# Two heads per step in a fixed TensorE order, and scores of the banded heads on all 128 rows

## The chip, the core and the metric

The kernel runs on one core of a Trainium2 chip. The metric is the device time of one execution in microseconds (us), the median of three runs. A run is followed by an execution under the hardware profiler, and the profile and the trace come from that one.

## What is computed

Two transformer blocks over 512 tokens of width 1024, in float32: a first block of two layers, then a second block of two layers which also carries 256 context tokens. The stages that matter here are the attention stages:

```python
# first block, each layer: 4 output heads, each over three dilated key sets; pooled and convolved branches beside them
br_a = multiscale_pool(a_in, pool_w[l], pool_scale[l]) @ w_branch_a[l]
br_b = (b_b * causal_dwconv(b_c * b_x, conv_b_w[l])) @ w_branch_b[l]
br_c = dilated_attention(q, k, v) @ w_branch_c[l]
# second block, layer 0: heads "a" (8 query heads, 2 key heads, banded, with a sink) and "b" (difference of two softmaxes)
s_loc = jnp.where(valid, einsum('bnqhgd,bnkhd->bhgnqk', qb, kb) * scale, NEG_INF)   # own block and its neighbours
s_ctx = einsum('bnqhgd,bchd->bhgnqc', qb, k_ctx) * scale
p_loc, p_ctx, _ = joint_softmax(s_loc, s_ctx, s_sink)
outs = einsum('bhqk,bkhd->bqhd', p[:, 0] - lam * p[:, 1], v)
# second block, layer 1: 16 latent heads over 768 keys (mla_attend)
```

## The kernel before

Every product of float32 data is made of three matmuls on two float32r parts, a high and a low one: high by high, low by high, high by low (`mm3`, lines 133 to 138). A head of the first three kinds is 64 wide, so a query block's scores contract over 64 of the array's 128 rows: rows 0 to 63 for one head, 64 to 127 for its neighbour.

An attention stage is a list of items, each a tuple of four functions: `qk` (scores into a PSUM tile S, two banks, and the row minimum on VectorE), `soft` (exponentials on ScalarE, normalisation on GpSimd), `tr` (`probs_T`, line 421: six or fewer TensorE transposes into two T tiles, the first copied out by ScalarE, the second by VectorE) and `pv` (probabilities by values, `pv_pair` for two heads side by side). `pipeline` (line 382) walks over the list with a delay for each function, and after each step lets a generator of other work (`Fill`, line 41) emit projections up to a budget of so many nanoseconds. `Fill.need` emits what is left of a piece that the next item needs. PSUM has eight banks: two S tiles, two T tiles of one bank and two "p" tiles of one bank, and the p tiles are shared by the projections, their transposes and the outputs of `pv`.

The order in which TensorE meets these instructions is not the one of the program: the framework's scheduler picks, from what it expects to be ready, by priority.

There are four such stages, in the order of time:

- `mix1` (lines 604 to 690), once in each layer of the first block: 16 items (two groups of heads p, four query blocks, two heads each), with the projections of the second group (`proj1`), the pooled branch (`pool_in`, `pool_out`) and the convolved branch as fill, in this order. `pool_in` goes through a chain on GpSimd and VectorE (lines 565 to 590); `pool_out` multiplies its results.
- the difference heads of `mix_ab` (`diff_items`): four heads h, each eight items over 768 keys (four query blocks, two maps m) and two items over the 256 context keys, with the projections `proj_ab` of the heads and of the banded groups 4 and 5 as fill.
- the banded heads of `mix_ab` (`window_items`): 32 items of two or three local blocks and two context blocks, then eight context items, with hardly any fill left (200 ns a step).
- `mix_mla`: 64 items with its own projections `proj_mla` as fill, 96 rows per head.

Of the kernel before, what the change touches and what calls it, by code (L numbers as in the profile page):

```python
# [78 lines left out]
class Net:  # L79
# [398 lines left out]
    def items1(self, p, g, fill, oT):  # L478
# [5 lines left out]
        def item(b, h):  # L484
            st = {}
            rows = slice(64 * h, 64 * h + 64)
            qs = slice(b * P, (b + 1) * P)

            def qk():
                if (b, h) == (0, 0):  # L490
                    fill.need(p)
                q0, k0, q12, k12 = g["q0"], g["k0"], g["q12"], g["k12"]
                ps = self.psum("S")
                self.mm3(ps[:, 0], (q0[rows, 0, qs], q0[rows, 1, qs]), (k0[rows, 0], k0[rows, 1]), True, True)
                for j in range(2):
                    o = ps[:, 1, j * P : (j + 1) * P]
                    mm(o, lhsT=q12[rows, j, qs], rhs=k12[rows, j, qs], start=True, stop=True)
                st["s"] = ps.rearrange("p a b -> p (a b)")[:, :768]
                st["nm"] = self.nmax(st["s"], mask=self.mask1[:, b])

            def soft():
                st["P"], r = self.exps(st["s"], st["nm"], 768)
                self.norm_probs(st["P"], r)

            def tr():
                sh[b, h] = self.probs_T(st["P"], 6)

            def pv():
# [7 lines left out]
                self.pv_pair(o, [sh[b, 0], sh[b, 1]], vs)  # L516
                self.copy(oT[:, qs], o)

            return (qk, soft, tr, pv if h else None)

        return [item(b, h) for b in range(4) for h in range(2)]
# [506 lines left out]

# [683 lines left out]
```

## Time and profile before

| what | us |
|---|---|
| runs | 3593.20, 3593.13, 3589.31 (median 3593.13) |
| the profiled execution, its own time | 3594.31 |
| its span, first to last instruction | 3592.5 |
| TensorE busy in the span | 3519.9 (98%) |
| VectorE, ScalarE, GpSimd busy | 1917.2 (53%), 1335.5 (37%), 429.1 (12%) |
| mean granted TensorE clock | 0.994 |

A matmul's duration in the trace goes from its start to a modelled end, and the next one starts before that end; what a matmul costs TensorE in a dense stretch is the distance between two starts. The 1.8 us between span and time lie outside the program's instructions.

### The profile page before, as it was taken

What the parts mean: (1) busy time and instruction counts of PE and PEld (TensorE: products, weight loads), DVE (VectorE), ACT (ScalarE), POOL (GpSimd) and SP (SyncE); (2) the same over time, 40 slices, a digit from 0 to 9 for tenths busy, and PEclk for the clock granted to TensorE, in tenths of its full rate; (3) what the DMA queues carried; (4) which work ended last, traced back from release to release, by engine and by line L of the source; (5) the groups of instructions that cost most, each with busy time, mean ns of one, the idle gap of its engine ahead of it and who ended that gap; (6) DMA issues with size and microseconds to landing.
All of it is one profiled execution on the core that took longest, in us unless ns stands there. A gap on an engine that the chain in (4) does not pass through costs nothing.

```text
span 3592.5 us, 48260 instructions
## 1 busy us (share of the span) xinstructions
PE 3519.9 (98%) x19261; PEld 2994.1 (83%) x19261; DVE 1917.2 (53%) x3018; ACT 1335.5 (37%) x2372; POOL 429.1 (12%) x572
## 2 busy tenths in 40 slices
PE   8999999999999999999999999999999989999998
PEld 8877798888898778888878887888888878888887
DVE  4453357466534335666766666536663466753243
ACT  4432344332443324532344446332111356643222
POOL 0211111000102111200011122200000122220001
PEclk9999999999999999999999999999999999999999
DMA  4233334344322433354431112335443121022232
GB/s 129 83 129 94 100 112 141 106 144 135 103 66 93 135 94 124 121 167 150 131 107 40 36 48 77 125 93 168 132 132 103 46 80 33 25 89 87 90 102 86
DMA packets 110130, 364.02 MB, mean 101 GB/s; under 512 B 16617, under 2 KB 18209, under 8 KB 109905
## 3 DMA queue, kind: packets, MB, share of 16 engines
q1 hardware_dynamic: 109904, 360.94, 31.7%
q8 instruction: 151, 2.47, 0.3%
q14 instruction: 75, 0.61, 0.1%
HBM read 347.16 MB, written 13.73 MB: 100 GB/s over the span
## 4 chain that ended last, share of the span: by engine, by line
PE 90%; DVE 3%; ACT 2%; POOL 2%; DMA 1%; issue 1%; SPq 0%; ACTq 0%; POOLq 0%; DVEq 0%
PE ps L136 21%; PE ps L137 21%; PE ps L138 21%; PE p L136 4%; PE p L137 4%; PE p L138 4%; PE T L430 3%; PE p L444 3%; PE S L136 2%; PE S L137 1%; PE S L138 1%; DMA adaw<-in_ada_w_dram 1%; PE T L138 1%; PE T L136 1%; PE T L137 1%
## 5 line engine op out<-in xcount | busy, mean ns | idle before, releaser
L112 DVE TENSOR_TENSOR wlo<-raw,whi 128x1024 fp32r<-128x1024 f32 (+2 forms) x510 | 603.8, 1190 | 734.6 <-ACT whi L109 719.3
L109 ACT ACTIVATE whi<-raw 128x1024 fp32r<-128x1024 f32 (+2 forms) x510 | 518.1, 1019 | 1113.1 <-PE ps L137 710.2
L137 PE MATMUL ps<-hTlo,whi 128*128 128x512 f32 (+1 forms) x2048 | 757.6, 370 | 4.1 <-DVE hTlo L177 4.0
L136 PE MATMUL ps<-hThi,whi 128*128 128x512 f32 (+1 forms) x2048 | 757.7, 371 | 2.7 <-ACT hThi L109 1.4
L138 PE MATMUL ps<-hThi,wlo 128*128 128x512 f32 (+1 forms) x2048 | 756.7, 370 | 0.0
L136 PEld LDWEIGHTS ps<-hThi,whi 128*128 128x128 f32 x2048 | 385.8, 189 | 73.0 <-issue 3.5
L137 PEld LDWEIGHTS ps<-hTlo,whi 128*128 128x128 f32 x2048 | 386.5, 189 | 69.9 <-DVE hTlo L177 4.5
L138 PEld LDWEIGHTS ps<-hThi,wlo 128*128 128x128 f32 x2048 | 386.3, 189 | 65.2
L930 DVE SCALAR_TENSOR_TENSOR acc<-adaw,cs,acc 128x1024 f32<-128x1024 f32 x168 | 209.4, 1279 | 14.6 <-DMA adaw<-in_ada_w_dram 14.3
L136 PE MATMUL ps<-whi,a 128*128 128x512 f32 x440 | 170.9, 392 | 0.7 <-ACT a L109 0.7
L138 PE MATMUL ps<-whi,a 128*128 128x512 f32 x440 | 170.6, 390 | 0.0
L137 PE MATMUL ps<-wlo,a 128*128 128x512 f32 x440 | 170.6, 390 | 0.0
L136 PE MATMUL p<-whi,hThi 128*128 128x384 f32 x464 | 163.1, 352 | 7.5 <-ACT hThi L175 3.1
L137 PE MATMUL p<-wlo,hThi 128*128 128x384 f32 x464 | 158.2, 341 | 4.7 <-DVE wlo L112 4.7
L154 POOL TENSOR_SCALAR rstd<-ms 128x1 f32<-128x1 f32 x78 | 24.1, 309 | 1137.9 <-ACT junk L152 1122.7
L138 PE MATMUL p<-whi,hTlo 128*128 128x384 f32 x464 | 158.2, 341 | 0.7 <-DVE hTlo L112 0.7
L262 DVE TENSOR_TENSOR y<-y,ps 128x1024 f32<-128x1024 f32 x88 | 106.6, 1218 | 85.7 <-PE ps L138 85.4
L136 PE MATMUL ps<-whi,act 128*128 128x512 f32 x352 | 138.2, 395 | 0.0
L137 PE MATMUL ps<-wlo,act 128*128 128x512 f32 x352 | 137.2, 392 | 0.0
L138 PE MATMUL ps<-whi,act 128*128 128x512 f32 x352 | 136.3, 390 | 0.0
L420 POOL TENSOR_SCALAR g<-g,den 128x768 f32<-128x768 f32 (+3 forms) x88 | 74.6, 850 | 424.3 <-DVE den L416 375.6
L109 ACT ACTIVATE PT<-T 128x384 f32<-128x384 f32 (+2 forms) x160 | 74.4, 465 | 111.6 <-PE T L430 109.6
(407 smaller groups left out, 6830.8 us busy)
## 6 DMA issues: line engine op xcount, KB each, us to landing
raw<-in_ffn_w_dram SPq DMA_DIRECT2D x132, 512.0 KB
adaw<-in_ada_w_dram SPq DMA_DIRECT2D x96, 512.0 KB
raw<-in_w_up_dram SPq DMA_DIRECT2D x88, 512.0 KB
raw<-in_w_gate_dram SPq DMA_DIRECT2D x48, 512.0 KB
raw<-in_w_down_dram SPq DMA_DIRECT2D x44, 512.0 KB
raw<-in_w_qkv_dram SPq DMA_DIRECT2D x48, 384.0 KB
xd<-x SPq DMA_DIRECT2D x20, 512.0 KB
raw<-in_w_conv_dram SPq DMA_DIRECT2D x18, 512.0 KB
```

What stands on the lines that cost most here:

```text
L109: return self.nc.scalar.activation(out, in_, AF.Copy, scale=scale)
L112: return self.nc.vector.tensor_tensor(out, a, b, op=ALU.subtract)
L136: mm(ps, lhsT=l[0], rhs=r[0], start=first, stop=False)
L137: mm(ps, lhsT=l[0], rhs=r[1], start=False, stop=False)
L138: mm(ps, lhsT=l[1], rhs=r[0], start=False, stop=last)
L154: nc.gpsimd.tensor_scalar(r, ms, 1.0, EPS, op0=ALU.mult, op1=ALU.add)
L262: self.nc.vector.tensor_tensor(yps[t], yps[t], y, op=ALU.add)
L420: self.nc.gpsimd.tensor_scalar(Pt, Pt, r, 1.0, op0=ALU.mult, op1=ALU.mult)
L430: nc.tensor.transpose(ps[:, k * P : (k + 1) * P], Pt[:, (k0 + k) * P : (k0 + k + 1) * P], self.ident)
L444: self.nc.tensor.matmul(o[64 * h : 64 * h + 64], lhsT=vs(h, k), rhs=PTs[h][:, k], start=k == 0, stop=k == nk - 1)
L930: nc.vector.scalar_tensor_tensor(acc[r], w, c, acc[r], op0=ALU.mult, op1=ALU.add)
```

## The change

In all stages that use `pipeline`, TensorE now gets its instructions in the order in which the program emits them (`manual_schedule`). Within a step the order of the four functions is pv, qk, tr, soft, where it was qk, tr, soft, pv. An item may carry delays of its own.

In `mix1` and in the difference heads one item now covers both heads (both maps), and the matmuls of the two alternate, rows 0 to 63 and rows 64 to 127 in turn (`mm3_two`). The two context items of a difference head become one. In `mix1` the projections of the second group are no longer fill: they are emitted in one piece ahead of that group's first scores; the convolved branch comes first in the fill and the pooled one last. In `mix_ab` each projection is added to the fill when the head before it begins, and the last one with the last context item.

In the banded heads the two parts of a query lie one above the other: rows of the head's own half hold the high part, the other half the low part (`stacked`). The keys stand in two copies, one for each key head, each with the high part in both halves of one plane, and the low part in both halves of the other (`keys_twice`). Two matmuls over 128 rows then give the scores in place of three over 64; the low by low product is added by this.

`mix_mla` and its items are not edited, but go through the same `pipeline`.

```diff
+    def mm3_two(self, pss, ls, rs):
+        for i, j in ((0, 0), (0, 1), (1, 0)):
+            for ps, l, r in zip(pss, ls, rs):
+                self.nc.tensor.matmul(ps, lhsT=l[i], rhs=r[j], start=(i, j) == (0, 0), stop=i == 1)
...
     def pipeline(self, items, fill, ns, steps=(0, 1, 2, 3)):
-        for i in range(len(items) + steps[-1]):
-            for s in (0, 2, 1, 3):
-                j = i - steps[s]
-                if 0 <= j < len(items) and items[j][s] is not None:
-                    items[j][s]()
-            fill.run(ns if isinstance(ns, (int, float)) else ns[min(i, len(items) - 1)])
+        own = [it[4] if len(it) > 4 else steps for it in items]
+        with self.tc.manual_schedule(engines={mybir.EngineType.PE}):
+            for i in range(max(j + o[3] for j, o in enumerate(own)) + 1):
+                for s in (3, 0, 2, 1):
+                    for j, it in enumerate(items):
+                        if j + own[j][s] == i and it[s] is not None:
+                            it[s]()
+                fill.run(ns if isinstance(ns, (int, float)) else ns[min(i, len(items) - 1)])
...
             def qk():    # items1
-                if (b, h) == (0, 0):
-                    fill.need(p)
+                if b == 0 and p:
+                    drain(proj)
...
-                self.mm3(ps[:, 0], (q0[rows, 0, qs], q0[rows, 1, qs]), (k0[rows, 0], k0[rows, 1]), True, True)
+                pss = [self.psum("S") for _ in both]
+                self.mm3_two([ps[:, 0] for ps in pss], [(q0[r, 0, qs], q0[r, 1, qs]) for r in both], [(k0[r, 0], k0[r, 1]) for r in both])
...
-                fill.add(1, self.proj1(l, 1, hT, gs[1], ("p",)))
+                proj = self.proj1(l, 1, hT, gs[1], ("p",))
+                fill.add("conv", self.conv_branch(l, hT, bF))
                 fill.add("pool", self.pool_in(l, hT, pooled))
-                fill.add("conv", self.conv_branch(l, hT, bF))
                 fill.add("pool", self.pool_out(l, pooled, aF))
-                self.pipeline(self.items1(0, gs[0], fill, oF[0]) + self.items1(1, gs[1], fill, oF[1]), fill, 7200, (0, 1, 2, 3))
+                items = self.items1(0, gs[0], None, oF[0]) + self.items1(1, gs[1], proj, oF[1])
+                self.pipeline(items, fill, [9000] * 4 + [8500] * 4, (0, 0, 1, 2))
...
+    def stacked(self, tok, col, tiles, dst, scale, tag):
+        tiles = list(tiles)
+        n = len(tiles) * P
+        yield 0.0
+        ps = self.psum(tag)[:, :n]
+        for j, t in enumerate(tiles):
+            self.nc.tensor.transpose(ps[:, j * P : (j + 1) * P], tok[:, t, col : col + P], self.ident)
+            yield 109
+        c = slice(tiles[0] * P, tiles[0] * P + n)
+        for h in range(2):
+            own, other = slice(64 * h, 64 * h + 64), slice(64 - 64 * h, 128 - 64 * h)
+            self.copy(dst[own, h, c], ps[own], scale=scale)
+            self.nc.vector.scalar_tensor_tensor(dst[other, h, c], ps[own], scale, f32(dst[own, h, c]), op0=ALU.mult, op1=ALU.subtract)
...
+    def keys_twice(self, g):
+        ks = (self.qk.tile([P, 2, 768], R, name="qk"),
+              self.work.tile([P, 6, 256], R, name="tok").rearrange("p a b -> p (a b)").rearrange("p (a b) -> p a b", a=2))
+        for tiles in ((4, 5), range(4)):
...
+            for kv, k in enumerate(ks):
+                own, other = slice(64 * kv, 64 * kv + 64), slice(64 - 64 * kv, 128 - 64 * kv)
+                self.split(k[own, 0, c], k[own, 1, c], ps[own])
+                self.copy(k[other, 0, c], ps[own])
+                self.sub(k[other, 1, c], ps[own], f32(k[own, 0, c]))
+        g["k", 0], g["k", 1] = ks
...
-            return (qk, soft, tr if m else None, (lambda: finish(t, 6)) if m else None)
+            return (qk, soft, tr, lambda: finish(t, 6), (0, 0, 2, 3))
...
+        def scores(ps, c, kv, q, keys):
+            k = g4["k", kv]
+            for i in range(2):
+                self.nc.tensor.matmul(ps, lhsT=qs(c)[:, kv, q], rhs=k[:, i, keys], start=i == 0, stop=i == 1)
...
-                self.mm3(ps[:, 0, c0:], ql, (kT[rows, 0, k0 * P : k1 * P], kT[rows, 1, k0 * P : k1 * P]), True, True)
-                self.mm3(ps[:, 1, :256], ql, (kT[rows, 0, 512:], kT[rows, 1, 512:]), True, True)
+                scores(ps[:, 0, c0:], c, kv, q, slice(k0 * P, k1 * P))
+                scores(ps[:, 1, :256], c, kv, q, slice(512, 768))
...
-                for i in range(1, 6):
-                    fill.add(i, self.proj_ab(hT, i, gs[i], ("p",)))
+                proj = [(i, self.proj_ab(hT, i, gs[i], ("p",))) for i in range(1, 6)]
                 items = []
                 for h in range(4):
-                    items += self.diff_items(h, gs[h], fill, oB[h])
+                    items += self.diff_items(h, gs[h], fill, oB[h], proj[h])
+                qk5 = items[-1][0]
+
+                def last():
+                    qk5()
+                    fill.add(*proj[4])
+                    fill.add(5, self.keys_twice(gs[4]))
+
+                items[-1] = (last,) + items[-1][1:]
                 n, oT = len(items), []
                 items += self.window_items(gs[4], gs[5], fill, oB, oT)
-                self.pipeline(items, fill, [3000] * n + [200] * (len(items) - n), (0, 1, 4, 5))
+                self.pipeline(items, fill, [6000] * 20 + [200] * (len(items) - n), (0, 1, 4, 5))
```

## Rows read from the trace of the kernel before

**Rows 1.** The page: busy time of each engine, share of the span.
```profile
PE 3519.9 (98%) x19261; PEld 2994.1 (83%) x19261; DVE 1917.2 (53%) x3018; ACT 1335.5 (37%) x2372; POOL 429.1 (12%) x572
...
PE 90%; DVE 3%; ACT 2%; POOL 2%; DMA 1%; issue 1%; SPq 0%; ACTq 0%; POOLq 0%; DVEq 0%
```

**Rows 2.** The four stages: stretch, length, busy time by engine, clock, DMA.
```profile
73.00:250.00 177.00, 174.26 (x1021) 148.49 (x1021) 79.60 (x159) 69.53 (x119) 31.94 (x43) 0.99 0.29 91
...
1903.00:2128.00 225.00, 220.77 (x1310) 196.37 (x1311) 140.10 (x343) 90.07 (x227) 36.84 (x64) 1.00 0.12 37
...
2140.00:2231.00 91.00, 89.78 (x731) 69.54 (x729) 65.20 (x251) 61.13 (x196) 30.83 (x48) 1.00 0.06 16
2949.00:3175.00 226.00, 222.91 (x1903) 195.98 (x1903) 157.46 (x333) 146.12 (x314) 60.03 (x64) 1.00 0.11 35
```

**Rows 3.** TensorE in order of time, a head's scores in mix1: start, duration.
```profile
201.76 0.49 PE L136 MATMUL S<-qk 64*128 64x512 f32 x1
...
202.33 0.39 PE L138 MATMUL S<-qk 64*128 64x512 f32 x1
202.56 0.60 PE L497 MATMUL S<-qk 64*128 64x128 f32 x4
203.10 0.87 PE L430 MATMUL T<-ident,g 128*128 128x128 f32 x6
```

**Rows 4.** TensorE in order of time, one map's scores, and a context item's.
```profile
1908.87 0.50 PE L136 MATMUL S<-qk 64*128 64x512 f32 x1
...
1910.11 0.44 PE L136 MATMUL p<-whi,hThi 128*128 128x384 f32 x1
...
1942.95 0.39 PE L136 MATMUL S<-qk 64*128 64x256 f32 x2
...
1943.29 0.28 PE L138 MATMUL S<-qk 64*128 64x256 f32 x2
1943.51 1.60 PE L1068 MATMUL p<-v,PT 128*128 128x128 f32 x12
```

**Rows 5.** TensorE in order of time, two banded items' scores.
```profile
2176.45 0.44 PE L136 MATMUL S<-qk 64*128 64x384 f32 x1
...
2177.53 0.77 PE L430 MATMUL T<-ident,big 128*128 128x128 f32 x5
...
2199.41 0.38 PE L136 MATMUL S<-qk 64*128 64x256 f32 x1
...
2200.31 0.66 PE L430 MATMUL T<-ident,g 128*128 128x128 f32 x4
```

**Rows 6.** The last pooled chain of layer 0: ScalarE, GpSimd, VectorE, in order of time.
```profile
174.44 0.57 ACT L109 ACTIVATE t<-p 128x512 f32<-128x512 f32 x1
...
180.09 1.03 POOL L578 TENSOR_TENSOR t<-t 128x504 f32<-128x504 f32 x1
...
182.21 0.75 DVE L586 SCALAR_TENSOR_TENSOR t<-t,poolc,t 128x512 f32<-128x512 f32 x1
```

**Rows 7.** Two stretches inside mix1: length, busy time by engine, clock.
```profile
126.00:129.00 3.00, 1.82 (x13) 1.40 (x11) 2.88 (x7) 1.99 (x5) 1.73 (x1) 1.00 0.31 42
129.00:132.40 3.40, 3.40 (x12) 3.00 (x13) 0.73 (x3) 1.64 (x4) 0.91 (x2) 0.50 0.29 118
```

**Rows 8.** Evacuations of transposes: count, min/median/max ns; then mix1's rotation.
```profile
L109 ACT ACTIVATE qk<-p x24: 377/412/633, 1902.1 to 2133.4; 128x256 fp32r<-128x256 f32 x13, 128x512 fp32r<-128x512 f32 x11
L120 DVE SCALAR_TENSOR_TENSOR qk<-p,qk x24: 406/423/693, 1902.8 to 2134.0; 128x256 fp32r<-128x256 f32 x13, 128x512 fp32r<-128x512 f32 x11
...
L458 DVE TENSOR_TENSOR ropeA<-tok,cos 128x96 f32<-128x96 f32 x8 | 2.1, 258 | 18.1 <-ACT tok L109 18.1
```

**Rows 9.** An undisturbed pv, then two behind their own item's transposes: start, duration, idle.
```profile
203.90 1.53 PE L444 MATMUL p<-PT,vt 128*64 128x128 f32 x24
...
248.66 0.55 PE L444 MATMUL p<-PT,vt 128*64 128x128 f32 x6 [0.90 <-ACT PT L109]
...
3170.95 1.89 PE L444 MATMUL p<-PT,v 128*64 128x128 f32 x24
```

More of the change, by code (lines that the diff above doesn't have):

```diff
@@ L514, in vs @@
                     return v[:, k if k < 4 else b, c : c + 64]
-                self.pv_pair(o, [sh[b, 0], sh[b, 1]], vs)
+                self.pv_pair(o, sh[b], vs)
                 self.copy(oT[:, qs], o)
-            return (qk, soft, tr, pv if h else None)
-        return [item(b, h) for b in range(4) for h in range(2)]
+            return (qk, soft, tr, pv)
+        return [item(b) for b in range(4)]
     def shifts(self, dst, src, k):
@@ L1043, in proj_ab, with diff_items @@
         sc = -(64 ** -0.5)
-        lst = [("a", tok, 0, sc), ("b", tok, P, 1.0 if i < 4 else sc)] + ([("c", v, 0, 1.0)] if i == 4 else [])
+        lst = [("a", tok, 0, sc), ("b", tok, P, 1.0 if i < 4 else sc)]
         for n, src, col, s in lst:
             g[n] = self.qk.tile([P, 2, 768], R, name="qk")
-            yield from self.transposed(src, col, (4, 5), g[n], s, tag=tags[0])
-            yield from self.transposed(src, col, range(4), g[n], s, tag=tags[-1])
+            to = self.transposed if i < 4 else self.stacked
+            yield from to(src, col, (4, 5), g[n], s, tag=tags[0])
+            yield from to(src, col, range(4), g[n], s, tag=tags[-1])
         g["v"] = v
-    def diff_items(self, h, g, fill, oB):
+    def keys_twice(self, g):
+        ks = (self.qk.tile([P, 2, 768], R, name="qk"),
+              self.work.tile([P, 6, 256], R, name="tok").rearrange("p a b -> p (a b)").rearrange("p (a b) -> p a b", a=2))
+        for tiles in ((4, 5), range(4)):
+            n = len(tiles) * P
+            yield 0.0
+            ps = self.psum("p")[:, :n]
+            for j, t in enumerate(tiles):
+                self.nc.tensor.transpose(ps[:, j * P : (j + 1) * P], g["v"][:, t], self.ident)
+                yield 109
+            c = slice(tiles[0] * P, tiles[0] * P + n)
+            for kv, k in enumerate(ks):
[4 more added lines that the diff above has]
+        g["k", 0], g["k", 1] = ks
+    def diff_items(self, h, g, fill, oB, after):
         nc = self.nc
@@ new lines, in ctx_item, with qk, soft @@
+        def ctx_item():
+            st = {}
+            def qk():
+                qT, kT = g["a"], g["b"]
+                both = [slice(0, 64), slice(64, 128)]
+                for t in (4, 5):
+                    q = slice(t * P, (t + 1) * P)
+                    ps = self.psum("S")
+                    st[t] = ps, self.sm.tile([P, 2], F32, name="nm2")
+                    self.mm3_two([ps[:, m, :256] for m in range(2)], [(qT[r, 0, q], qT[r, 1, q]) for r in both],
+                                 [(kT[r, 0, 512:], kT[r, 1, 512:]) for r in both])
+                for ps, nm in st.values():
+                    nc.vector.tensor_reduce(nm, ps[:, :, :256], axis=AX.X, op=ALU.min)
+            def soft():
+                for t, (ps, nm) in st.items():
+                    sh[t] = [self.exps(ps[:, m, :256], nm[:, m : m + 1], 256) for m in range(2)]
@@ L1121, in diff_items @@
-        return [item(t, m, t == 0 and m == 0) for t in range(4) for m in range(2)] + [ctx_item(t) for t in (4, 5)]
+                for t in st:
+                    sh["T", t] = self.probs_T(sh[t][0][0], 2)
+            return (qk, soft, tr, lambda: [finish(t, 2) for t in st], (0, 0, 2, 3))
+        return [item(t) for t in range(4)] + [ctx_item()]
     def diff_T(self, oB, oT):
@@ L1184, in qk @@
                 for c in range(2):
-                    qT = qs(2 * half + c)
-                    self.mm3(st["s"][:, c], (qT[rows, 0, q], qT[rows, 1, q]), (kT[rows, 0, 512:], kT[rows, 1, 512:]), True, True)
+                    scores(st["s"][:, c], 2 * half + c, kv, q, slice(512, 768))
             def soft():
```

73 lines of the change are left out of this document (27 added, 46 removed).

## The prediction

> **What bounds the kernel now.** I read the page first. TensorE is busy for 98% of the span and carries 90% of the chain that ended last, and VectorE, the next, is at 53% [rows 1]. The windows by stage say the same of each attention stage: TensorE is full in all four, the rest at 40 to 72% [rows 2] (layer 1's mix1 repeats layer 0's). Then the order of time on TensorE, by distances between starts. So time taken from TensorE is time gained, as long as nothing else comes late; and the order that TensorE has now leaves almost no waits. The change saves matmuls and gives that order up. The sum is the one against the other.
>
> **What it saves.** A head's scores in mix1 take 1.34 us from their first start to the next kind of work [rows 3]. Three starts of 512 columns lie 0.23 apart; the first takes 0.10 more, and so does the way back, each time the array changes between 64 and 128 rows. That two heads on different rows run at once is in the trace already: in a context item the scheduler has put the two maps side by side, six matmuls in three steps, 0.56 us for both [rows 4]. So a pair costs what one costs, plus one step of 0.11 for the float32 products, whose two passes per head overlap with the neighbour's but for one: 1.45. Eight pairs in each of two layers: 16 x (2.68 - 1.45) = 19.7 us. A map of the difference heads takes 1.24 us [rows 4], a pair 1.27: 16 x 1.21 = 19.4, and joining two context items saves one way there and back, 4 x 0.2 = 0.8. A banded item takes 1.08 us with three local blocks and 0.90 with two [rows 5]; two matmuls in place of three, without any change of rows, are 0.59 (2 x 0.17 and 2 x 0.12) and 0.48. 16 x 0.49 + 16 x 0.42, and eight context items at 0.42: 18.0. Together 57.9 us.
>
> The waits that mix1 has now go too, since its projections are no longer cut up: 1.2 us idle in 126 to 129 and, behind it, 3.4 us at a clock of 0.50, the lower of the two levels, 1.2 GHz, which costs 1.7 [rows 7]. Twice 2.9 is 5.8.
>
> **What the banded stage can't take.** In its 91 us VectorE works for 65 and ScalarE for 61 [rows 2], and none of that goes. TensorE falls to 73, plus waits. A score tile also has to go through VectorE's minimum and ScalarE's exponential before the item after next may start, and there are two. I let 8 of the 18 us arrive: +10.0, between 0 and 18. The Trainium skill says in TensorEngine Tiling (Array Packing), Performance Considerations, that tiling speeds up TensorE but not the evacuation of PSUM, which may then bound. The 65 us of VectorE bear that out only in part; if it held in full, the 18 us would be gone and the sum 8 us higher.
>
> **What the fixed order costs.** Each place is one where the program's next TensorE instruction isn't ready.
>
> *pool_out in mix1.* By the budgets, steps 0 to 3 take seven of nine chains of the convolved branch, and step 7 takes the last kc of `pool_in` and then at once `pool_out`. Its second output needs the third pooled tile. That chain takes 8.5 us from ScalarE's copy to VectorE's last sum [rows 6], then a split of 0.6 + 0.7 [rows 8], with pauses 10.2. Ready in between are twelve matmuls of 0.23 [rows 3], 2.7 us. So 7.5 us of wait, and 1 to 2 more where the two normalisations of the last pair stand on GpSimd in its way: 8.5, and another 1.7 for the half clock behind a wait [rows 7]. Two layers: +20.4, between 15 and 26. Before, the scheduler put other work there.
>
> *proj1's transposes.* After a group's last tile they wait for the copy and four rotation instructions of 0.26 [rows 8], 1.3 us, and the third transpose group waits for the first one's p tile, 1.0: 2.3, for q and k, in two layers: +9, between 4 and 14.
>
> *proj_ab's transposes.* They fall into the step of the context item, where the budget leaves only them: 1.3 us of TensorE work, needing two p tiles in turn, with four copies and four subtractions of 0.4 to 0.7 [rows 8], behind the four exponentials of the context item on ScalarE. The next head's scores wait for the last of them. Copies first gives 2.2 us a head, exponentials first 3.9; 3 x 3 = +9, between 4 and 14.
>
> *Groups 4 and 5 and the keys.* `stacked` doubles the copies and subtractions, and `keys_twice` takes eight of each. All of that is emitted in one piece ahead of the first banded scores: some 8 us on ScalarE and 9 on VectorE, on the instructions' own lengths [rows 8], beside 2 us of transposes. 7 us of wait there, 4 at group 4, and 1 to fill the banded pipeline, less the 1 us that stands there now: +11, between 5 and 16.
>
> *pv behind its own transposes.* With pv first in a step and tr last, the banded stage and `mix_mla` (delays 4 and 5, 3 and 4) put an item's pv right behind its transposes unless fill comes between. The trace has that place at two tails: where ScalarE is free the 24 matmuls take 1.89 us against 1.53, where it isn't they wait 0.9 [rows 9]. By the budgets 19 of the 32 pv of `mix_mla` have no fill; at 0.35 that is 6.6. The banded ones are in the 10 above. *proj_mla's own evacuations* (two splits for each half tile) are waited for once in seven projections, some 0.8 us: 5.4. Together +12, between 5 and 25.
>
> Sum: -57.9 - 5.8 + 10.0 + 20.4 + 9 + 9 + 11 + 12 = +7.7. The profiled execution took 3594.3, its span and 1.8 around it, and lies 1.2 above the median; on the median the sum is **3601**. The DMA queue keeps its transfers; their order follows the new fill, and at 6 to 29% of the engines' time [rows 2] I cost that at nothing; a late weight would show as a wait of TensorE for `raw`.
>
> **Rivals.**
> - *The waits are covered better than I cost them* (evacuations come first in their queues, the banded stage takes most of its gain): all costs at their lower ends but the banded one at 4 give -63.7 + 4 + 15 + 4 + 4 + 5 + 5 = -27: 3566. For it: VectorE and ScalarE are idle for a quarter or more in every stage [rows 2]. Against: the pooled chain is serial.
> - *The order isn't as fixed as it reads*: the scheduler fills these waits with the next stage's work. Then the savings stay, less the banded stage's 10: -53.7, 3539. Against: nothing in the edit allows it.
> - *The evacuations become the bound*: the banded stage gives nothing (+8 over the forecast), each of the 19 pv waits 0.9 (+10), the other places go half the way to their upper ends (+10): 3629, slower. It decides from where VectorE's and ScalarE's work in a step is longer than TensorE's. The skill's sentence on PSUM speaks for this one.
> - *The pairs don't run at once at 512 columns*: 40 us of the saving go, 3641. The trace shows pairs at 256 columns only [rows 4].
>
> **How the numbers follow.** Forecast, that the order gives back about what the pairs save: 0.46. Rivals in order: 0.28, 0.06, 0.16, 0.04. A measurement tells about 0.2% from no change, 7 us. Around 3601 the forecast's bounds spread by some 10 us: of its 0.46, 0.05 is faster, 0.19 within, 0.22 slower; the first rival gives 0.03 to within. Faster 0.36, same 0.22, slower 0.42. For 8 in 10 the range runs from 3560, just past the first rival, to 3630, the third.
>
> **What would show it.** Paired scores: two starts some 10 ns apart, 0.23 to the next two; banded scores of two matmuls with no 0.10 ahead. In mix1, one idle stretch of 7 to 10 us ahead of `pool_out`'s second output, ended by VectorE's split, with half clock after it; 2 us waits after proj1's q and k. Between the difference and the banded heads a gap of some 7 us ended by the keys' subtraction. In `mix_mla` many short waits of pv for ScalarE's PT copy. I am wrong if the gap ahead of `pool_out` isn't there, or if the banded stage shrinks by all of its 18 us.

## The result, and the profile after

The changed kernel takes 3683.6 us (median; 3681.0 to 3689.4), the kernel before, run beside it, 3591.6: a ratio of 1.0259 [1.0241, 1.0277], 92 us slower. That is above the range; the forecast of 3601 lies 83 us below it. The profiled execution took 3689.36 us, 5.8 more than the median; its span is 3687.6, and the stages below therefore add up to 95 us and not to 92. One execution of a kernel below (pairs apart) was in a slower state, 5013.7 us, and is left out of its median. In everything below a stage runs from its first matmul on TensorE to the first of the next one, leading projections included, and stages of two kernels are compared in their profiled executions.

| stage | before | after | measured | predicted |
|---|---|---|---|---|
| mix1, layer 0 | 239.9 | 260.8 | +20.9 | both layers: |
| mix1, layer 1 | 236.4 | 258.8 | +22.4 | +3.9 |
| mix_ab | 365.0 | 382.5 | +17.5 | -8.2 |
| mix_mla | 240.0 | 276.8 | +36.8 | +12 |
| all else | 2511.2 | 2508.7 | -2.5 | 0 |

The page of after, its engines and the engines' shares of the chain that ended last (against [rows 1]):

```profile
PE 3506.0 (95%) x19181; PEld 2987.8 (81%) x19181; DVE 1930.5 (52%) x3032; ACT 1345.0 (36%) x2386; POOL 422.3 (11%) x572
...
PE 79%; DVE 5%; ACT 4%; issue 2%; POOL 2%; DMA 1%; SPq 0%; ACTq 0%; POOLq 0%; DVEq 0%
```

TensorE is busy for 14 us less, where 58 us of matmuls were saved, and its share of the chain fell from 90 to 79%. The windows of the four stages of after say why (columns as in [rows 2]: length, then busy time by engine, then the granted clock):

```profile
73.00:271.00 198.00, 170.69 (x1023) 144.96 (x1024) 79.90 (x161) 68.65 (x122) 30.94 (x44) 0.95 0.26 80
1020.00:1220.00 200.00, 172.73 (x1024) 146.89 (x1021) 77.59 (x160) 68.31 (x119) 28.89 (x40) 0.94 0.24 76
1948.00:2292.00 344.00, 300.60 (x2042) 264.55 (x2042) 225.52 (x637) 167.35 (x460) 71.45 (x120) 0.94 0.11 35
3008.00:3268.00 260.00, 234.68 (x1896) 204.57 (x1895) 160.71 (x330) 147.84 (x313) 57.75 (x64) 0.96 0.09 28
```

and mix_ab as a whole in the kernel before:

```profile
1903.00:2231.00 328.00, 321.85 (x2122) 275.52 (x2122) 215.19 (x623) 159.13 (x446) 71.27 (x120) 1.00 0.12 36
```

Read length less busy time as TensorE's idle time. It was 2.7 us in a layer of mix1, 6.2 in mix_ab and 3.1 in mix_mla ([rows 2] and the row above); now it is 27.3, 27.3, 43.4 and 25.3: some 109 us of new waits. Then read the clock: 0.95 over 198 us means 20 us at 0.50 and the rest at 1.00, and the four stages together have some 106 us at 0.50, the 1.2 GHz level. In mix_mla the matmuls are the same as before, and TensorE is still busy 12 us longer, [rows 2] against the last window of after: 21 us at half rate account for 10 of them. What TensorE waited for, over the whole span of after (total, times, longest):

```profile
PE T L439 <- ACT PT L109: 35.5, 40, 3.0
PE p L136 <- ACT qk L109: 12.4, 2, 6.3
PE p L1037 <- DVE qk L120: 11.4, 6, 3.4
PE p L1050 <- DVE qk L1056: 10.2, 4, 4.9
...
PE p L1037 <- DVE hClo L120: 7.1, 3, 2.8
PE p L453 <- DVE kTlo L112: 6.4, 3, 2.1
PE p L478 <- DVE tok L470: 5.5, 4, 1.4
PE p L1037 <- DVE kTlo L112: 4.7, 2, 2.7
PE p L478 <- ACT qk L109: 4.3, 4, 1.4
```

The first line, the largest, is a wait that the prediction does not have. It is a transpose waiting for a T tile to be copied out. In TensorE's order of time, in a step of mix1 (start, duration, idle before):

```profile
189.06 0.96 PE L144 MATMUL S<-qk 64*128 64x512 f32 x6
189.86 0.61 PE L506 MATMUL S<-qk 64*128 64x128 f32 x8
190.39 0.88 PE L439 MATMUL T<-ident,g 128*128 128x128 f32 x6
193.38 1.26 PE L439 MATMUL T<-ident,yg 128*128 128x128 f32 x6 [2.11 <-ACT PT L109]
```

The pair's scores take 1.33 us from first start to the transposes, 1.45 had been worked out. Then come six transposes of the first head, into both T tiles, and the six of the second find no tile free until ScalarE has copied the first one out. A head's `tr` needs two tiles, a pair's four, and there are two.

How long the second head stands depends on what ScalarE has ahead of that copy. In the step shown it is a weight's split, which itself stood for the transfer:

```profile
191.80 1.06 ACT L109 ACTIVATE whi<-raw 128x1024 fp32r<-128x1024 f32 x1 [2.14 <-DMA raw<-in_w_pool_dram]
192.76 0.47 ACT L109 ACTIVATE PT<-T 128x384 f32<-128x384 f32 x1
```

In layer 0 the wait of transposes for PT copies is 15.6 us in 14 pieces. Nine are of 0.3 to 0.9 us, 5 in all: the copy alone, or the copy behind one exponential. The other five, 10 us, are those in which something late stood ahead of the copy on ScalarE: this transfer (2.1), the pooled chain, which it had to wait for (3.0 and 1.0), and an exponential that had waited for its row minimum (2.1 and 2.0).

### The profile page after: what moved, and what is told of

The parts are those of the page before. It is cut to its first block, busy times and chain, and to the rows that moved or that the text cites. A ratio compares the mean times of both kernels' runs of the same rounds, so it can differ in the third digit from the quotient of the medians.

```text
span 3687.6 us, 48153 instructions
## 1 busy us (share of the span) xinstructions
PE 3506.0 (95%) x19181; PEld 2987.8 (81%) x19181; DVE 1930.5 (52%) x3032; ACT 1345.0 (36%) x2386; POOL 422.3 (11%) x572
## 4 chain that ended last, share of the span: by engine, by line
PE 79%; DVE 5%; ACT 4%; issue 2%; POOL 2%; DMA 1%; SPq 0%; ACTq 0%; POOLq 0%; DVEq 0%
PE ps L136 20%; PE ps L137 20%; PE ps L138 20%; PE p L136 3%; PE p L137 3%; PE p L138 3%; PE p L453 2%; PE T L439 2%; DVE wlo L112 1%; DMA adaw<-in_ada_w_dram 1%; PE p L1117 1%; PE S L136 1%; PE S L144 1%; ACT whi L109 1%; PE S L138 1%
```

## The experiments

Every kernel was timed against the kernel before, on the same chip. Theory A of the first runs: the edits save what was worked out and the fixed order gives it back in waits. The rival: the edits themselves ask for more than any order can cover.

**The order alone.** One line:

```
-        with self.tc.manual_schedule(engines={mybir.EngineType.PE}):
+        with ExitStack():
```

> The changed kernel, but TensorE's order is left to the scheduler again (the fixed order taken away, everything else kept: pairs, stacked scores, own delays, pv first in a step). Theory A, the fixed order alone costs the time: the matmuls saved (39 us of pairs, 10 to 18 us of banded scores) arrive and the waits go, 3530 to 3560 us, and the stretches at a clock of 0.50 fall from 25 back to about 10. Theory B, the edits themselves cost it (a pair takes both score tiles and wants four T tiles at once, so that no order of TensorE covers the evacuations): at least half of the 92 us stays, 3630 us or more, with the waits of transposes for the PT copies still near 35 us.

Measured: 3607.2 us, 1.0047 [1.0032, 1.0062]. Neither theory. The order costs 76 us, but without it the edits still lose 17 where by the prediction's terms they should have gained 54 (57.9 and 5.8, less 10.0). The stages came to 241, 238, 368 and 246 us: even in the scheduler's order layer 0 of mix1 waits 6.1 us ahead of `pool_out`, since by then little else is left to do, and 5.1 us with transposes for PT copies.

**mix_mla alone**, with the old order of functions and the scheduler there:

```
+        with self.tc.manual_schedule(engines={mybir.EngineType.PE}) if fixed else ExitStack():
+                for s in (3, 0, 2, 1) if fixed else (0, 2, 1, 3):
-                    self.pipeline(items, fill, 2600, (0, 1, 3, 4))
+                    self.pipeline(items, fill, 2600, (0, 1, 3, 4), fixed=False)
```

> The changed kernel, but mix_mla, whose items the change does not edit, has its old order of functions and the scheduler's order again; the other stages are as in the change. Theory A, the fixed order costs in this stage by itself: its 261 us go back to 224, so 3684 - 37 = 3647 us (3640 to 3655). Theory B, the stage is slow because of what the stages ahead leave behind (clock, late weights): under 10 us of change, 3675 us or more.

Measured: 3650.3 us, 1.0166 [1.0149, 1.0183]; the stage is at 239.6. Theory A: 33 us of the loss come from a stage whose items the change doesn't touch. The edit undoes two things there, the fixed order and the new order of functions; in the first run above, where only the fixed order is gone, the stage takes 246 us, so most of its 37 us, some 31, are the fixed order and some 6 the order of functions.

**pool_out behind the last pv.**

```
-                fill.add("pool", self.pool_out(l, pooled, aF))
...
                 fill.drain()
+                drain(self.pool_out(l, pooled, aF))
```

> The changed kernel, but pool_out is taken out of mix1's fill and emitted behind the last pv of the stage, so that two pv and the last pair's transposes stand between the pooled chain and its reader. Theory A, the wait ahead of pool_out is a plain wait that some 5 us of other TensorE work can cover: the 6.4 us wait shrinks to 1 or 2 in each layer, and with half of the slow clock behind it 5 to 7 us a layer are gained, 3670 to 3675 us. Theory B, the last pair's own chain (scores, exponentials, normalisation, transposes, pv) is as long as the pooled one, so the wait only moves to the last transposes: under 3 us a layer, 3679 us or more.

Measured: 3671.8 us, 1.0227 [1.0212, 1.0242], 12 less than the change; each layer is 8 us shorter. Theory A. The place itself, in after, where `pool_out`'s second output starts, and the clock behind it:

```profile
253.37 0.40 PE L138 MATMUL p<-qk,wlo 128*128 128x512 f32 x1
260.07 0.80 PE L136 MATMUL p<-qk,whi 128*128 128x512 f32 x1 [6.30 <-ACT qk L109]
...
260.10:265.30 5.20, 4.86 (x13) 3.13 (x15) 1.05 (x2) 1.40 (x2) 0.00 (x0) 0.50 0.34 101
```

The matmul behind the wait takes 0.80 us against 0.40 for the one ahead of it.

**Pairs not alternated.** One head's three matmuls are issued, then the other's:

```
-        for i, j in ((0, 0), (0, 1), (1, 0)):
-            for ps, l, r in zip(pss, ls, rs):
+        for ps, l, r in zip(pss, ls, rs):
+            for i, j in ((0, 0), (0, 1), (1, 0)):
```

> The changed kernel, but the matmuls of two heads no longer alternate: one head's scores are issued, then the other's, in mix1 and in the difference heads (the context items too); order, items and all else are as in the change. Theory A, the alternation saves the 39 us that were worked out for it, in the fixed order too: 3684 + 39 = 3723 us (3715 to 3730). Theory B, in this order TensorE waits for evacuations anyway, so that a shorter score block only makes the next wait longer: a good part is hidden, 3685 to 3705 us.

Measured: 3682.4 us, 1.0256 [1.0241, 1.0272]: no difference at all, and neither theory, because the edit did not undo the pairs. The six matmuls of 512 columns of one pair, in after and then in this run, with first and last start:

```profile
L144 PE MATMUL S<-qk x6: 390/390/496, 189.1 to 189.6; 64*128 64x512 f32 x6
```

```profile
L144 PE MATMUL S<-qk x6: 390/392/496, 188.2 to 188.7; 64*128 64x512 f32 x6
```

Six starts lie within 0.6 us in both. With 0.23 between two starts on the same rows [rows 3], one head's three and then the other's would need about 0.9 or more, if each waited for the one issued ahead of it. So the two heads run at once without alternation, as neighbours in the order. A better undoing:

**Pairs apart.** The pv of an earlier pair stands between the two heads' scores:

```
+                for s in (0, 3, 2, 1) if i < apart else (3, 0, 2, 1):
+                    if s == 2:      # the second head's scores, behind pv
+                        for f in other:
+                            f()
...
+                head(0)
+                return lambda: head(1)
```

> The changed kernel, but a pair's two heads are no longer neighbours in TensorE's order: the pv of an earlier pair stands between the first head's scores and the second's, in 12 of mix1's 16 pairs and 13 of the 16 of the difference heads (the first ones have no pv yet). Nothing else is changed. Theory A, two heads on different rows run at once when they are neighbours, and that is worth 1.2 us a pair also here: 25 x 1.2 = 30 us slower, 3714 us (3705 to 3720). Theory B, TensorE waits for evacuations in those steps anyway, and a shorter score block makes the wait longer: under 12 us slower, 3684 to 3696 us.

Measured: 3710.2 us, 1.0329 [1.0312, 1.0346], 27 slower than the change. But the place splits: nearly all of it is in mix_ab (382.5 to 407.3), more than the 16 us that 13 pairs come to at 1.2 (what the rest is isn't shown), and mix1 loses nothing (260.2 and 258.3). Theory A for the one, B for the other. In layer 0 of mix1 the waits of transposes for PT copies are 5.3 us in place of 15.6, so what the pairs save there had gone into waits.

**The second head's transposes later**, after half of the step's fill:

```
-                sh[b] = [self.probs_T(Pt, 6) for Pt in st["P"]]
+                sh[b] = [self.probs_T(st["P"][0], 6)]
+                return lambda: sh[b].append(self.probs_T(st["P"][1], 6))
```

> The changed kernel, but in mix1 the transposes of a pair's second head come after half of the step's fill in place of right behind those of the first head. Theory A, the second head's transposes wait because the two T tiles are still being copied out, and only for that: 8 to 12 us a layer go, half clock included, 3660 to 3668 us, and the waits of transposes for PT copies in mix1 all but vanish. Theory B, the copies themselves are late (queued behind exponentials and the fill's own evacuations), so the waits turn up at the next reader: under 3 us a layer, 3678 us or more.

Measured: 3650.3 us, 1.0166 [1.0151, 1.0182], 33 less than the change; mix1 is at 244.4 and 239.0. Theory A, and more than it said. TensorE's waits over the whole span of this run:

```profile
PE p L136 <- ACT qk L109: 18.2, 2, 9.1
...
PE T L448 <- ACT PT L109: 4.9, 14, 0.4
```

35.5 us have become 4.9; `pool_out` now waits 9.1 in place of 6.3, since TensorE comes to it earlier.

**pv a step later** in the banded stage and in mix_mla:

```
-                self.pipeline(items, fill, [6000] * 20 + [200] * (len(items) - n), (0, 1, 4, 5))
+                self.pipeline(items, fill, [6000] * 20 + [200] * (len(items) - n), (0, 1, 4, 6))
-                    self.pipeline(items, fill, 2600, (0, 1, 3, 4))
+                    self.pipeline(items, fill, 2600, (0, 1, 3, 5))
```

> The changed kernel, but in the banded stage and in mix_mla the product with the values comes one step later (delays 0, 1, 4, 6 and 0, 1, 3, 5), so that the next item's scores and transposes stand between an item's transposes and its pv. Theory A, with pv first in a step TensorE goes round in a loop with ScalarE (scores, minimum, exponential, then the PT copy behind it, then pv), 4.78 us for a pair of three local blocks of which 0.95 are a wait: about 10 us of the banded stage and 15 of the 37 in mix_mla come back, 3658 us (3645 to 3668). Theory B, VectorE and ScalarE are what those stages are bound by, whatever the order: the wait moves to the scores, under 8 us, 3676 us or more.

Measured: 3675.1 us, 1.0231 [1.0214, 1.0247], 8.5 less: between the two. From the first banded pv to the last it is 78.2 us in place of 86.9 (before: 88.2), so in the banded stage theory A holds. The loop, in after, one pair of three local blocks on TensorE, then ScalarE's work at the same time, then the window of that pair:

```profile
2242.63 0.86 PE L1194 MATMUL S<-qk 128*128 128x384 f32 x4
2243.33 0.71 PE L439 MATMUL T<-ident,g 128*128 128x128 f32 x5
2243.79 0.83 PE L1194 MATMUL S<-tok,qk 128*128 128x384 f32 x4
2244.55 0.74 PE L439 MATMUL T<-ident,yg 128*128 128x128 f32 x5
2245.22 0.43 PE L453 MATMUL p<-PT,v 128*64 128x128 f32 x2
2246.18 1.31 PE L453 MATMUL p<-PT,v 128*64 128x128 f32 x18 [0.53 <-ACT PT L109]
2247.41 0.85 PE L1194 MATMUL S<-qk 128*128 128x384 f32 x4
```

```profile
2244.86 0.79 ACT L420 ACTIVATE g<-S,nm 128x640 f32<-128x640 f32 x1 [0.45 <-DVE nm L412]
2245.55 0.19 ACT L420 ACTIVATION_READ_ACCUMULATOR g<-S,nm 128x1 f32 x1
2245.64 0.48 ACT L109 ACTIVATE PT<-T 128x384 f32<-128x384 f32 x1
```

```profile
2242.63:2247.41 4.78, 4.25 (x39) 3.56 (x38) 3.45 (x14) 3.18 (x9) 1.60 (x3) 1.00 0.01 2
```

The pv of such a pair and the next pair's first scores, in the kernel before:

```profile
2180.00 1.31 PE L444 MATMUL p<-PT,v 128*64 128x128 f32 x20
2181.24 0.44 PE L136 MATMUL S<-qk 64*128 64x384 f32 x1
```

The period is 4.78 us, where before it was 4.79 (from 2176.45 [rows 5] to 2181.24): the scores are shorter, 0.70 against 1.08 for the first item, scores and transposes of both items together by 0.96, and pv takes 2.19 in place of 1.24, because the PT copy sits behind an exponential on ScalarE. VectorE works for 3.45 us of the period and ScalarE for 3.18, both less than TensorE. In mix_mla the step brought only 5 us, so there the cause is another; its waits moved to `p L1037 <- DVE kTlo`, 15.7 us.

**A pause in mix_mla's projections.**

```
                 self.split(kT[0][:64, h, c : c + n], kT[1][:64, h, c : c + n], ps[64 * h : 64 * h + 64])
+            yield 2600.0
```

> The changed kernel, but in mix_mla's projections the fill pauses for one step after each half tile of keys, so that an item's own scores and transposes stand between a p tile's evacuation and the matmul that takes the tile next. Theory A, what mix_mla lost is TensorE waiting for those p tiles in the middle of its fill (and the clock behind the waits): 10 to 18 of its 37 us come back, 3666 to 3674 us. Theory B, it is the items' own pv, transposes and scores that wait for their evacuations in a fixed order: under 5 us, 3679 us or more.

Measured: 3665.5 us, 1.0205 [1.019, 1.022], 18 less; the stage is at 258.3, and its clock back at 1.00. Theory A. The pattern in after: the last matmul of the keys' projection, then a pv that takes the p tile the keys are still being split out of:

```profile
3126.85 0.28 PE L138 MATMUL p<-klhi,wlo 128*128 128x256 f32 x1
3129.26 2.15 PE L453 MATMUL p<-PT,v 128*64 128x128 f32 x17 [2.13 <-DVE kTlo L112]
```

**All four covers together**, in the fixed order everywhere.

> The changed kernel in its fixed order everywhere, with four covers together: pool_out late, the second head's transposes after half of the fill, pv a step later in the banded stage and mix_mla, and the pause in mix_mla's projections. Alone they gave 12, 33, 8 and 18 us. Theory A, the change lost its time in separate waits, each with its own reader: the four add up to 71, 3613 us (3605 to 3622). Theory B, they share one cause (evacuations late as a whole): 40 us or less, 3643 us or more.

Measured: 3605.0 us, 1.0042 [1.0028, 1.0057]: 79 us less than the change, against 72 for the sum of the four alone. Theory A: separate waits, each with its own reader. mix1 is now at 236.7 and 232.5, under the kernel before; mix_ab is at 373.4 and mix_mla at 252.1, above it.

**The transposes of proj_ab spread**, on top of the four covers, and then mix_mla as before too (the edit shown above for it):

```
+        for c in self.tok_proj(hT, self.I["ab_w_in_2"][i], tiles, 384, evac, tags=tags):
+            if not c:
+                seen += 1
+                if seen == 5:    # ahead of the last tile
...
+                    yield from to(tok, 0, range(4), g["a"], sc, tag=tags[-1])
+            yield c
...
+        yield from to(tok, P, range(4), g["b"], sb, tag=tags[-1])
+        yield from to(tok, 0, (4, 5), g["a"], sc, tag=tags[0])
+        yield from to(tok, P, (4, 5), g["b"], sb, tag=tags[0])
```

> The run with all four covers, in the fixed order everywhere, and besides the transposes of proj_ab spread: those of the four query blocks of "a" come ahead of the last tile's projection, those of "b" right behind it, the short ones of the context tiles last. Theory A, the transposes at the end of each projection are the fifth separate wait (some 21 us in the trace of that run for the heads' and the groups' qk, and half clock behind it): 15 to 25 us less, 3580 to 3590 us, so at or under the kernel before. Theory B, the next head's scores wait for the last short transposes just as long: 5 us or less, 3600 us or more.

> The same, and mix_mla, whose items the change does not touch, in its old order (functions and scheduler). Theory A: mix_mla goes from 252 to 240 us, 12 us less than the run before this one, 3568 to 3578 us, faster than both kernels; what the saved matmuls are worth then shows as the distance to the kernel before, 13 to 23 of the 58 us. Theory B, the spread transposes bring nothing: 3593 us, no faster than the kernel before.

Measured: 3608.9 us, 1.0046 [1.0034, 1.0059], and 3594.8, 1.0012 [1.0003, 1.0021]. Theory B in both: the waits did not go, three of 3.8 us took the place of six that summed to the same, and the second kernel is 4 us slower than the kernel before. What each head waits for, in after, on TensorE and on ScalarE:

```profile
1985.85 0.94 PE L1037 MATMUL p<-ident,tok 128*128 128x128 f32 x6
1990.19 0.69 PE L1037 MATMUL p<-ident,tok 128*128 128x128 f32 x2 [3.41 <-DVE qk L120]
1991.40 1.11 PE L1037 MATMUL p<-ident,tok 128*128 128x128 f32 x4 [0.52 <-DVE qk L120]
1992.31 1.06 PE L1117 MATMUL p<-v,PT 128*128 128x128 f32 x4
```

```profile
1987.60 0.47 ACT L420 ACTIVATE big<-S,nm 128x256 f32<-128x256 f32 x1
...
1988.50 0.49 ACT L420 ACTIVATE yg<-S,nm 128x256 f32<-128x256 f32 x1
...
1988.95 0.89 ACT L109 ACTIVATE qk<-p 128x256 fp32r<-128x256 f32 x2
```

The copy that frees the p tile is queued behind the context item's exponentials, whichever transposes are last. mix_mla gave its 12 us (252.0 to 239.9), as expected.

**One edit at a time on the kernel before.** First all edits of the arithmetic in its frame (scheduler, old function order, old fill), then the stacked scores alone, the difference heads' pairs alone, and mix1 alone with its two covers. The edits are pieces of the change's diff; what differs from it:

```
+            for s in (0, 2, 1, 3):                            # the first
+                self.pipeline(items, fill, 14400, (0, 0, 1, 2))
...
+                fill.add(5, self.keys_twice(gs[4]))           # the second, behind the five projections
...
-                    fill.add(*after)                          # the third: projections are fill from the start
```

> Pairs and stacked scores of the change in the frame of the kernel before: the scheduler picks TensorE's order, a step goes scores, transposes, exponentials, pv, and in mix1 the second group's projections, the pooled branch and the convolved branch are fill in the old order, 14400 ns a pair. Theory A, the edits of the arithmetic are sound and only the order and the fill's new sequence cost: mix1 falls by 8 to 10 us a layer below the 240 of before, mix_ab stays where it was without the fixed order (368), mix_mla is at 240: 3570 to 3580 us. Theory B, a pair by itself cannot be covered (four T tiles wanted at once, both score tiles taken): mix1 stays at 238 or more, 3588 us or more.

> The kernel before with the banded heads' stacked scores alone (two matmuls over 128 rows, queries stacked, keys twice), in the scheduler's order and with the old fill; no pairs. Theory A, TensorE bounds the banded stage, and the 18 us of matmuls saved there arrive but for some 8 us of added evacuations ahead of it: 3581 us (3576 to 3586). Theory B, the stage goes at the pace of the loop through VectorE and ScalarE as soon as TensorE's part shrinks, and the added evacuations come on top: 3590 to 3600 us.

> The kernel before with the difference heads' pairs alone (one item for both maps, alternating matmuls, one context item), in the scheduler's order and with the projections as fill from the start, as before; no stacked scores. Theory A, the pairs save 1.2 us each and the freely ordered projections cover what a pair makes TensorE wait for: 16 x 1.2 = 19, of which 12 or more arrive, 3572 to 3580 us. Theory B, a pair takes both score tiles, so that the next pair's scores wait for both exponentials and the gain goes into that: 5 us or less, 3586 us or more.

> The kernel before with the change's mix1 alone (pairs, fixed order there only, the change's fill sequence), and with both of mix1's waits covered: the second head's transposes come after half of the step's fill, and pool_out behind the last pv. The other stages are those of before. Theory A, the two waits are all that kept mix1's saving away: its two layers come to about 236 and 231 us, against 240 and 236 before, 3581 us (3577 to 3586). Theory B, with those waits gone the next one is as long (the second group's transposes, the last pair's own chain): mix1 stays at 240, 3588 us or more.

Measured, in this order: 3601.0 us, 1.0029 [1.0019, 1.004]; 3594.3, 1.001 [1.0, 1.002]; 3585.7, 0.9985 [0.9976, 0.9994]; 3587.9, 0.999 [0.9981, 0.9999]. In the first, mix1 stays at 244.7 and 239.9: theory B, pairs with their transposes in one piece aren't covered by the scheduler either (8.7 and 9.0 us of waits of transposes for PT copies). Theory B in the second as well: the stacked scores gain 8 us between the first and the last banded pv (80.4 against 88.2) and lose 14 ahead of them (252.4 us from the first difference scores to the first banded pv, against 238.5), where the doubled evacuations stand. (That profiled execution took 3599.9 us, 5.5 above its median, so the 14 is rather too high.) The difference heads' pairs lie near theory B: mix_ab is 3 us shorter, the whole 5. mix1's pairs gain 3, between the two theories.

**Together.** The pairs of both stages with two more covers in mix1, the same with the stacked scores, and the pairs of both without those covers, which are:

```
+            yield None                       # proj1, ahead of q's and of k's transposes
...
+                    for c in proj:
+                        if c is None:
+                            self.fill1.chain()    # one chain of the convolved branch
```

> Pairs without the rest: mix1 as in the run with the change's mix1 alone (second head's transposes after half of the fill, pool_out behind the last pv), and besides a chain of the convolved branch ahead of the second group's q transposes and one ahead of its k transposes; the difference heads paired in the scheduler's order; banded heads and mix_mla as before. Theory A, each cover brings what its wait cost: mix1 loses another 3 to 5 us a layer, the difference heads keep the 4 us that they gained alone, 3577 us (3572 to 3582), faster than both kernels. Theory B, what is taken from the wait is added elsewhere in the step: 3583 to 3588 us.

> The same with the banded heads' stacked scores and the doubled keys added, in the scheduler's order and with the projections as fill from the start. Theory A, the stacking loses as it did alone (8 us gained in the steady banded part, 14 lost on evacuations ahead of it): 4 to 7 us above the run without it. Theory B, with paired difference heads TensorE is shorter ahead of the banded heads, so still less of these evacuations is covered: 8 to 12 us above it. Theory C, the joined items leave VectorE and ScalarE earlier, and the stacking becomes a gain: below it.

> Pairs without the rest, and without the convolved chains ahead of the second group's transposes: the change's mix1 with its two covers, in the fixed order there only, and the difference heads paired in the scheduler's order; banded heads and mix_mla as before. Theory A, the two gains measured alone (3 and 5 us) add: 3583 us (3579 to 3586), a little faster than both kernels. Theory B, they are within what one schedule differs from the next (the run with the chains added came out at 3590): 3587 to 3592 us.

Measured: 3589.7 us, 1.0001 [0.9991, 1.0011]; 3588.1, 0.9993 [0.9984, 1.0001]; 3582.8, 0.9976 [0.9966, 0.9986]. The last is theory A: the two gains measured alone add up, and this kernel is 8 us faster than the kernel before. The first is above even theory B, but its executions spread from 3582.3 to 3604.3 us; against that spread the second, 1.6 us lower, decides nothing.

The first one's mix_ab came out at 370.9 us and the last one's at 360.3, with the same items and fill. It is not the order: in both traces the 2311 matmuls of the stage follow each other in the same order. Up to the first banded pv the two are level (255.3 us from the first matmul into an S tile); from there to the last banded pv it is 101.4 against 90.5. The windows of the same 112 matmuls, where they part, in the first and then in the last:

```profile
2140.21:2164.37 24.16, 24.16 (x113) 19.50 (x112) 10.80 (x43) 9.64 (x29) 5.26 (x7) 0.51 0.00 1
```

```profile
2137.54:2151.15 13.61, 13.61 (x112) 11.11 (x112) 10.36 (x41) 9.18 (x29) 4.47 (x6) 1.00 0.01 2
```

TensorE was busy throughout; 24.2 us in the one at a granted clock of 0.51, 13.6 in the other at 1.00, are the whole difference. The longest wait ahead of it was 0.9 us in the first and 0.7 in the last. Why the clock fell in one of the two isn't shown, nor whether the spread of the first run's times is the same thing, since each run has one trace. So the first run says little of its two added covers, and the second is better held against the last, which has the same difference heads: in their traces the stacked scores take 10 us off the banded part (80.8 against 90.5) and add 13 ahead of it (268.0 against 255.3), and mix_ab is at 363.1 against 360.3. That is nearer to theory A than to C.

## Why the prediction was wrong

- *What bounds the kernel: right.* TensorE, and an order that leaves it no waits. The forecast's mechanism, that the fixed order gives the saving back, is what happened; the working had its sign right (+7.7 on the profiled execution) and its size wrong by 87 us there. What failed is the part on what the fixed order costs: 39 of the 87 us are in mix1, 26 in mix_ab and 25 in mix_mla, and all else is 2.5 shorter. Neither of the signs that the prediction named for being wrong came: the gap ahead of `pool_out` is there, and the banded stage did not shrink by 18 us.
- *The pairs' price: right.* 1.33 us a pair against 1.45; setting two heads apart costs 25 us in mix_ab.
- *Step missing: the second head's transposes.* The prediction followed the change's matmuls, fill and function order, but not the number of T tiles that a joined item takes at once. 36 us in the two layers of mix1 (16.4 + 19.8, from the split of `tr`), out of the 39 that mix1 came out above its term. Transfers were costed at nothing, with a wait of TensorE for `raw` as the sign of a late weight; the one late weight among these waits (2.1 us) shows a step further on, as a PT copy behind that weight's split.
- *`pool_out`: the place right, the wait a little high.* 8.5 us worked out, 6.3 measured, with half clock behind it, as said, though the wait ended with ScalarE's part of the split and not with VectorE's. But it isn't the fixed order's alone: the free order has it as well (6.1). proj1's transposes: 4.5 us a layer worked out, 4.9 measured.
- *`mix_mla`: mis-sized by 25 us.* Its own evacuations had been put at 0.8 us in each of seven projections. Eight waits, three for the queries' split (hClo) and five for the keys' (kTlo), make 7.1, 6.4 and 4.7 us, 2.3 each, and the stage has 21 us at 0.50. The pv waits for PT copies, which the prediction named as the sign to look for in this stage, are hardly there: 2.0 us in three for VectorE's copy, none for ScalarE's.
- *The banded stage: right in direction, too hopeful.* 8 of 18 us were let through; 1.3 arrived. The upper bound held: the saved matmul time went into a loop through ScalarE. With pv a step later 10 arrived.
- *proj_ab, groups and keys: mis-sized.* The waits are 3.8 us a head, 11.4 in three: "exponentials first", worked out at 3.9, was the case and not the mean. With the matmuls at half clock behind them it is 6.5, 6.2 and 6.2 us (the first from 1985.85 to 1992.31), less 1.3 of work each 15, over the upper bound of 14. The waits of the groups' and the keys' transposes and of the first banded scores are some 16 us (6.8 at group 4, 8.7 from group 5 on), and 2.3 more where the banded pipeline fills, against 11, clock not counted.
- *The clock: mis-sized throughout.* The prediction put a price on it at one place, 1.7 us a layer. In the rows stretches at 0.50 stand behind new waits, long and short: 106 us in all, up to half of it lost. The sum priced waits and left out the slower matmuls after them.
- *The rivals.* The third, that evacuations become the bound, was nearest. It decides, as the prediction put it, where VectorE's and ScalarE's work in a step is longer than TensorE's. That was not what decided: both are busy for only 34 to 66% of the four stages after the change, and in the banded period shown for 3.45 and 3.18 us against TensorE's 4.25. A single late copy was enough, because in a fixed order everything behind it waits. The Trainium skill says in TensorEngine Tiling (Array Packing), Performance Considerations, that tiling speeds up TensorE but not the evacuation of PSUM, and that the copies may become the bottleneck. The traces agree in part: TensorE waited for evacuations, 35.5 us for PT copies alone, but the engines that evacuate weren't full, as those shares show.

## What to carry to other kernels

When items are joined or an order is fixed, count for each step the PSUM tiles that it takes in a row against the tiles there are, and for each tile the queue in which its evacuation stands: a wait appears wherever the next taker comes before that evacuation, however idle the engines are on average. Work saved on the bounding engine arrives only where no such wait is behind it, so the covers (work from elsewhere put between a tile's evacuation and its next taker) belong in the same change as the saving. A wait of TensorE is to be priced with the slower matmuls behind it, not with its own length alone.

## What was not expected of the hardware

Two heads' matmuls on different rows ran at once although all three of one head were issued ahead of the other's: six starts within 0.6 us, the same as with alternation, and the same time for the kernel (3682.4 against 3683.6 us). The Trainium skill, in TensorE: Matmul & The Clock Gate, Part 3, states that matmuls start strictly in the order of issue; by that, as an estimate with the step of [rows 3], the pair would have taken five steps of 0.23 us and not three. No run here tells which head each start belongs to, so what is shown is the time of the six, not their order.

And the granted clock was low where waits were short: in mix_mla TensorE was idle for 25 of 260 us, in pieces of at most 2.8, and 21 us of the stage were granted at 0.50; with the pause in its projections the clock was 1.00. But 24 us at 0.50 also stood in the banded stage of one execution, behind a wait of 0.9 us, while another with the same order of matmuls stayed at 1.00. So one execution can differ from the next by some 10 us, and a stage's time is to be compared with the clock beside it.
